# Attention on one Trainium2 core: queries and keys of a pair of heads rounded and split by one operation each, and the last two heads' probabilities turned on TensorE

## The chip, the cores and the metric

The kernel runs on one core of a Trainium2 chip. A core has five engines with instruction queues of their own: TensorE (PE) multiplies matrices, VectorE (DVE) and ScalarE (ACT) work element by element, GpSimd (POOL) and SyncE (SP) here mostly issue transfers, which sixteen DMA engines carry out. The engines meet only at semaphores. On-chip data lies in SBUF, with 128 partitions (rows); TensorE writes to PSUM. The metric is the device time of one execution in microseconds (us). Lower is better.

## The reference

The program is a trunk of four residual layers over 512 tokens of width 1024, in float32: attention, a squared-ReLU MLP, a Griffin recurrent block, another MLP. The change touches attention alone:

```python
qkv = einsum('bsd,de->bse', rmsnorm(h), w_qkv)      # 16 heads of 64
s = einsum('bqhd,bkhd->bhqk', q_c, k_band) * 64**-0.5 + bias
p = softmax(where(key_pos >= 0, s, -1e30))           # own chunk of 64 and the 8 before
o = einsum('bhqk,bkhd->bqhd', p, v_band)
h = h + einsum('bsd,de->bse', o, w_o)
```

With 512 tokens, a query sees all keys up to the end of its own chunk.

## The kernel before

A float32 product is made of three matmuls in a rounded format (fp32r): each operand is split in a high half H (a rounded copy, made on ScalarE) and a low half L (what the rounding left, a subtraction on VectorE), and `mm3` (L288 to L290) adds H·H, L·H and H·L in PSUM. Weights are fetched raw and split in the same way (L179, L184), a few tiles ahead of their use.

Heads go in pairs, since two heads of 64 fill the 128 partitions. A pair p's projected queries and keys come out of `qk_steps`, and `q_out` and `k_out` finish them. `q_out` scales the product to a tile tq (L384), then makes for each head of the pair a 64-row cast (L388) and a 64-row subtraction (L389): a head's q tile has its high half in its own 64 rows and its low half in the other 64. `k_out` scales to tk (L394) and makes four tiles: for each head kh and kl, by a 64-row cast (L399) and subtraction (L400) in the head's own rows; two transfers a head, issued by SyncE (L401, L402), copy them to the other 64 rows. So a score needs only two matmuls a piece: kl against q and kh against q (L483, L484).

`score(h)` makes the scores of head h for four blocks of 128 queries (128 to 512 keys: eight matmuls), adds the bias while taking the maximum (L491, VectorE), takes the exponential and its sum (L498, ScalarE), the reciprocal (L502), divides on ScalarE (L505), turns 32 x 32 blocks on VectorE (L507) and moves the blocks to their places by sixteen transfers (L510), eight issued by SyncE and eight by GpSimd. `split_p(h)` splits these probabilities in pH (L519) and pL (L520). `weigh(h)` multiplies them by v: ten matmuls (L530, L531), then the low and high v halves' results are added (ax L536, o L537), and behind the second head of a pair o is split in oH and oL (L541, L542).

The order is that of a loop over i (from L616 on). Step i makes the scores of head i, fills TensorE with some queued projection work, splits head i-2, weighs head i-3, and fills again. `fill(n)` takes work from one queue: v of pairs 0 to 3 (v0), queries and keys of pairs 2 to 6, v1, queries and keys of pair 7, then the output projection (woA for pairs 0 to 3; wo0, wo1 and woB for pairs 4 to 7). n is FILL up to step 10 and LATE from then on; each item also names the head whose scores or weighing must have been made (`at`). The last output products wait for pair 7: `wo_close` adds it to four opened accumulators. The program's order is the input of the framework's scheduler, which fixes every engine's order when the kernel is built, and may let an instruction pass one that is expected to wait. PSUM has four tiles for projections (tag mm) and four for attention (tag at).

Of the kernel before, what the change touches and what calls it, by code (L numbers as in the profile page):

```python
# [13 lines left out]
ALU = mybir.AluOpType  # L14
# [11 lines left out]
FILL, LATE, LAG = 11.5, 8, 3  # L26
# [9 lines left out]
def f(ap):  # L36
    return ap.bitcast(F32)
# [3 lines left out]
def trunk(ctx: ExitStack, tc: tile.TileContext, xT, cols, gfin, win, wqkv, wo, rwin, rga, rgx, rwo, w1, w2, out):  # L41
# [260 lines left out]
    class Norm:  # L302
# [8 lines left out]
        def square(self, k):  # L311
            if self.acc is None:
                self.both = self.pool.tile([P, 2, T], F32, name=f"{self.name}acc", tag="nn")
                self.acc = self.both[:, 0]
# [14 lines left out]
        def flat(self):  # L329
            ss = atp(f"{self.name}ss")  # L330
            aH, aL = (wk.tile([P, T], F32R, name=f"{self.name}a{i}", tag="nsq", bufs=2) for i in range(2))
            S.copy(aH, self.acc)
            V.tensor_sub(aL, self.acc, f(aH))
            PE.matmul(ss, ones.bitcast(F32R), aH, start=True, stop=False)
            PE.matmul(ss, ones.bitcast(F32R), aL, start=False, stop=True)
            r = self.both[:, 1]
            S.activation(r, ss, AF.Sqrt, bias=epsb, scale=1.0 / D)
            V.reciprocal(r, r)
            return r
# [26 lines left out]
    with ExitStack() as actx:  # L366
# [14 lines left out]

        def q_out(p, acc):
            tmp = wk.tile([P, T], F32, name=f"tq{p}", tag="nsq", bufs=2)
            V.scalar_tensor_tensor(tmp, acc, HD**-0.5, r0, ALU.mult, ALU.mult)  # L384
            for hh in range(2):
                own, oth = HALF[hh], HALF[1 - hh]
                t_ = ab.tile([P, T], F32R, name=f"q{p}{hh}", tag=f"q{hh}", bufs=2)
                S.copy(t_[own], tmp[own])  # L388
                V.tensor_sub(t_[oth], tmp[own], f(t_[own]))  # L389
                q[2 * p + hh] = t_  # L390

        def k_out(p, acc):
            tmp = wk.tile([P, T], F32, name=f"tk{p}", tag="nsq", bufs=2)
            V.tensor_mul(tmp, acc, r0)  # L394
            for hh in range(2):
                own, oth = HALF[hh], HALF[1 - hh]
                kh = ab.tile([P, T], F32R, name=f"kh{p}{hh}", tag=f"kh{hh}", bufs=2)
                kl = ab.tile([P, T], F32R, name=f"kl{p}{hh}", tag=f"kl{hh}", bufs=2)
# [3 lines left out]
                nc.sync.dma_start(f(kl[oth]), f(kl[own]))  # L402
# [70 lines left out]
        def score(h):  # L473
# [11 lines left out]
            for t in range(4):  # L485
                n = (t + 1) * P
                wide = pt[:, seg[t] : seg[t] + n], sc[t], b[:, h % 4, T - n :]
                if t == 1:
# [13 lines left out]
            V.reciprocal(sm, sm)  # L502
            for t in range(4):
# [10 lines left out]
            pts[h] = pt  # L514

        def split_p(h):
            pt = pts.pop(h)
            pH, pL = (a2.tile([P, 10 * P], F32R, name=f"p{n}{h}", tag=f"p{n}", bufs=1) for n in "HL")
            S.copy(pH, pt)  # L519
# [3 lines left out]
        def weigh(h):  # L523
# [3 lines left out]
            for n, (kt, s0, s1, by, t) in enumerate(pieces):  # L527
                vv = vt[p // 2][:, kt, p % 2, 2 * hh : 2 * hh + 2, :].rearrange("p s d -> p (s d)")
                x = oa.rearrange("p (s i a) -> p s i a", i=4, a=32)[:, t : t + len(range(s0, s1, by))]
                PE.matmul(x, vv, pL[:, s0:s1:by], start=n == 0, stop=False, skip_group_check=True)  # L530
                PE.matmul(x, vv, pH[:, s0:s1:by], start=False, stop=n == 4, skip_group_check=True)  # L531
# [51 lines left out]
        def qk(p):  # L583
            return [(f"q{p}", qk_steps(p, q_out), ("s", 2 * p - 3)), (f"k{p}", qk_steps(p, k_out), ("s", 2 * p - 3))]
# [11 lines left out]
        def step():  # L596
            try:
                credit[0] -= next(queue[0][1])
            except StopIteration:
                queue.pop(0)  # L600

        def fill(n):
            credit[0] = min(credit[0], 3) + n
            while credit[0] > 0 and queue and at[queue[0][2][0]] >= queue[0][2][1]:
                step()
# [11 lines left out]
        for i in range(NH + LAG):  # L617
# [11 lines left out]
            if 0 <= i - LAG + 1 < NH:  # L629
                split_p(i - LAG + 1)  # L630
            if 0 <= i - LAG < NH:
                if i - LAG == 13:
                    need("woA")
                need(f"v{(i - LAG) // 8}")
                weigh(i - LAG)
                if i - LAG == 7:
                    residual("h")
                    for k in range(KT):
                        nc.sync.dma_start(hT[k], xT[k * P : (k + 1) * P, :])
                at["w"] = i - LAG  # L640
            fill(n)
        need("woB")
# [645 lines left out]
```

## Time and profile before

| | us |
|---|---|
| median of 3 runs (lowest, highest) | 1032.04 (1030.49, 1032.6) |
| the profiled execution | 1030.76 |
| its span, first to last instruction | 1029.0 |
| attention's stretch in it, about | 25 to 245 |

The mean granted TensorE clock is 0.992 over the span. A row of a timeline has the start, the duration, the engine, the line, the operation, the names of output and inputs, shapes and a count of equal instructions in a row; in brackets stands the time that the engine sat idle ahead of it, and what ended that. SPq is SyncE's queue, PEld TensorE's weight load. A grouped row has the busy time, the mean ns of one, and the idle time ahead of the group by what ended it.

### The profile page before, as it was taken

How to read it: one execution, taken by the hardware profiler on the slowest of the kernel's cores; microseconds unless marked ns; L12 is line 12 of the kernel's file. 1: busy time of each engine (PE TensorE's matmuls, PEld its weight loads, DVE VectorE, ACT ScalarE, POOL GpSimd, SP SyncE). 2: the span in 40 equal slices, each digit the busy share in tenths (PEclk: the TensorE clock that was granted, in tenths of full speed). 3: DMA queues.
4: the chain of work that ended last, by engine and by line, in shares of the span. 5: the costliest groups of instructions: out<-in, count | busy, mean ns of one | idle time of the engine just before them, and what ended most of it. 6: DMA issues, size and time to landing. Idle time of an engine off the chain costs nothing.

```text
span 1029.0 us, 15661 instructions
## 1 busy us (share of the span) xinstructions
PE 1006.7 (98%) x5634; PEld 882.0 (86%) x5634; DVE 865.8 (84%) x1142; ACT 692.5 (67%) x1052; POOL 163.4 (16%) x256
## 2 busy tenths in 40 slices
PE   9998999979999999999999999999999999999997
PEld 8887788768989999999988788888999999999986
DVE  7899988759789898698688989987789798698687
ACT  7688988546786566567567686646686567567565
POOL 1053443313111111111020000003111111111020
PEclk9999999989999999999999999999999999999999
DMA  8476775549838738828673412186838838838572
GB/s 271 125 203 182 196 189 174 132 129 230 240 62 223 208 60 217 215 52 213 204 143 100 129 63 72 52 256 177 223 58 229 206 64 213 214 56 210 144 164 82
DMA packets 135725, 164.15 MB, mean 160 GB/s; under 512 B 10592, under 2 KB 102752, under 8 KB 135648
## 3 DMA queue, kind: packets, MB, share of 16 engines
q1 hardware_dynamic: 108896, 119.43, 37.4%
q0 software_dynamic: 26176, 43.01, 23.2%
q8 instruction: 44, 0.72, 0.3%
q10 hardware_dynamic: 576, 0.72, 0.2%
q14 instruction: 33, 0.27, 0.1%
HBM read 123.27 MB, written 2.10 MB: 122 GB/s over the span
## 4 chain that ended last, share of the span: by engine, by line
PE 75%; DVE 10%; ACT 6%; DMA 5%; issue 2%; SPq 1%; POOL 0%; DVEq 0%; ACTq 0%; POOLq 0%
PE m L290 8%; PE m L289 8%; PE m L288 8%; PE x L288 5%; PE x L289 5%; PE x L290 5%; PE y L289 4%; PE y L288 4%; PE y L290 4%; DVE wl L184 2%; DMA p<-pt 1%; DMA b<-in_w 1%; PE ro L290 1%; PE yb L290 1%; PE yb L288 1%
## 5 line engine op out<-in xcount | busy, mean ns | idle before, releaser
L184 DVE TENSOR_TENSOR wl<-b,wh 128x1024 fp32r<-128x1024 f32 x112 | 135.5, 1220 | 37.1 <-ACT wh L179 37.1
L179 ACT CAST wh<-b 128x1024 fp32r<-128x1024 f32 x112 | 116.7, 1051 | 61.5 <-PE m L289 19.1
L290 PE MATMUL m<-rH,wl 128*128 128x256 f32 x448 | 125.9, 281 | 0.0
L289 PE MATMUL m<-rL,wh 128*128 128x256 f32 x448 | 125.8, 281 | 0.0
L288 PE MATMUL m<-rH,wh 128*128 128x256 f32 x448 | 125.7, 281 | 0.0
L290 PE MATMUL m<-hnH,wl 128*128 128x256 f32 x336 | 95.0, 283 | 0.0
L289 PE MATMUL m<-hnL,wh 128*128 128x256 f32 x336 | 95.0, 283 | 0.0
L288 PE MATMUL m<-hnH,wh 128*128 128x256 f32 x336 | 94.9, 282 | 0.0
L179 ACT CAST wh<-wr 128x1024 fp32r<-128x1024 f32 (+1 forms) x65 | 66.6, 1028 | 38.1 <-PE ro L289 7.0
L289 PEld LDWEIGHTS m<-rL,wh 128*128 128x128 f32 x448 | 85.0, 190 | 1.2
L184 DVE TENSOR_TENSOR wl<-wr,wh 128x1024 fp32r<-128x1024 f32 (+1 forms) x66 | 77.9, 1184 | 9.3 <-ACT wh L179 9.0
L288 PEld LDWEIGHTS m<-rH,wh 128*128 128x128 f32 x448 | 84.8, 189 | 1.0
L290 PEld LDWEIGHTS m<-rH,wl 128*128 128x128 f32 x448 | 84.9, 189 | 0.0
L510 POOL DMA_DIRECT2D p<-pt x128 | 62.8, 499 | 121.8 <-DVE pt L507 70.1
L179 ACT CAST wh<-u 128x1024 fp32r<-128x1024 f32 x56 | 58.2, 1049 | 28.8 <-PE x L290 16.9
L184 DVE TENSOR_TENSOR wl<-u,wh 128x1024 fp32r<-128x1024 f32 x56 | 67.6, 1219 | 3.4 <-ACT wh L179 3.4
L289 PEld LDWEIGHTS m<-hnL,wh 128*128 128x128 f32 x336 | 64.3, 191 | 0.8
L288 PEld LDWEIGHTS m<-hnH,wh 128*128 128x128 f32 x336 | 64.2, 191 | 0.8
L290 PEld LDWEIGHTS m<-hnH,wl 128*128 128x128 f32 x336 | 64.3, 191 | 0.0
L136 POOL DMA_DIRECT2D kept<-in_w x14 | 18.3, 1308 | 261.0 <-DMA wr<-in_w 146.8
L163 POOL DMA_DIRECT2D u<-in_w x14 | 18.4, 1313 | 226.1 <-ACT m L853 117.2
L288 PE MATMUL x<-wh,h 128*128 128x512 f32 (+1 forms) x132 | 51.0, 386 | 0.6 <-DVE d L1062 0.6
(384 smaller groups left out, 3017.5 us busy)
## 6 DMA issues: line engine op xcount, KB each, us to landing
b<-in_w SPq DMA_DIRECT2D x68, 512.0 KB, 6.1
b<-b POOLq DMA_DIRECT2D x36, 512.0 KB, 6.5
kept<-in_w SPq DMA_DIRECT2D x28, 512.0 KB, 3.8
u<-in_w SPq DMA_DIRECT2D x28, 512.0 KB, 6.1
wr<-in_wqkv SPq DMA_DIRECT2D x20, 512.0 KB, 4.8
wr<-in_rwin SPq DMA_DIRECT2D x16, 512.0 KB, 3.6
kept<-in_w POOLq DMA_DIRECT2D x14, 512.0 KB, 7.2
u<-in_w POOLq DMA_DIRECT2D x14, 512.0 KB, 7.5
```

Of the source, the lines that this page charges most:

```text
L136: G.dma_start(four(raw), rows(upper[key]["22"]), accum_op=ALU.add)
L163: G.dma_start(four(raws["us3"]), rows(upper[key]["21"]), accum_op=ALU.add)
L179: high = S.copy(H[:, :n], raw[:, :n])
L184: low = V.tensor_sub(L[:, :n], raw[:, :n], f(H[:, :n]))
L288: PE.matmul(acc, WH, XH, start=start, stop=False, skip_group_check=more)
L289: PE.matmul(acc, WH, XL, start=False, stop=False, skip_group_check=more)
L290: PE.matmul(acc, WL, XH, start=False, stop=stop, skip_group_check=more)
L510: (G if j % 2 else nc.sync).dma_start(pt[32 * j : 32 * j + 32, i * 320 : (i + 1) * 320], turned[32 * i : 32 * i + 32, j].rearrange("p s a ...
```

## The change

It has five parts.

1. `q_out` and `k_out` make one 128-row cast and one 128-row subtraction for a pair (new helper `halves`), where they made two of each over 64 rows. The halves are then carried to their places by transfers (`move`). For k these are six instead of four, on SyncE: the lower 64 rows of the pair's tile a hold head 0, the upper ones head 1; two moves for kh and two for kl copy head 1's rows to both halves of tile b, and only then may one move each copy head 0's rows over the upper rows of tile a. For q there are three, on GpSimd, where there were none; the low half lies in a tile of which there is only one (tag n0), and the third move overwrites rows that the first one reads.
2. The division of `score` is a function of its own (`divide`), which stands behind the second fill of a step.
3. Heads 14 and 15 (from TURNED on) are divided on VectorE by four operations. Ten 128 x 128 transposes on TensorE a head put the probabilities in three PSUM tiles (`turn`), from which three casts and three subtractions make pH and pL. The vector transpose and the sixteen transfers of these two heads are gone. `weigh` takes eight matmuls for them, of 512, 384, 256 and 128 columns.
4. Queries and keys in the fill queue no longer wait to start; only their last step (`out_`) waits for the scores of head 2p-3. The last two heads are split and weighed in the same step of the loop, with a fill between.
5. FILL goes from 11.5 to 11.7, LATE from 8 to 7.5. The norm's two tiles, which were one allocation, are two.

```diff
-FILL, LATE, LAG = 11.5, 8, 3
+FILL, LATE, TURNED = 11.7, 7.5, NH - 2
...
+        def halves(tmp, name, kinds):
+            both = []
+            for n in "hl":
+                t_ = [ab.tile([P, T], F32R, name=f"{name}{n}{i}", tag=k, bufs=1 if k == "n0" else 2) for i, k in enumerate(kinds[n])]
+                both.append(t_)
+            (h, l) = both
+            S.copy(h[0], tmp)
+            V.tensor_sub(l[0], tmp, f(h[0]))
+            return h, l
+
+        def move(queue, dst, i, src, j):
+            queue.dma_start(f(dst[HALF[i]]), f(src[HALF[j]]))
...
-            for hh in range(2):
-                own, oth = HALF[hh], HALF[1 - hh]
-                t_ = ab.tile([P, T], F32R, name=f"q{p}{hh}", tag=f"q{hh}", bufs=2)
-                S.copy(t_[own], tmp[own])
-                V.tensor_sub(t_[oth], tmp[own], f(t_[own]))
-                q[2 * p + hh] = t_
+            (a, b), (low,) = halves(tmp, f"q{p}", {"h": ("q0", "q1"), "l": ("n0",)})
+            move(G, b, 0, a, 1)
+            move(G, b, 1, low, 1)
+            move(G, a, 1, low, 0)
+            q[2 * p], q[2 * p + 1] = a, b
...
+            pairs = halves(tmp, f"k{p}", {"h": ("kh0", "kh1"), "l": ("kl0", "kl1")})
+            for a, b in pairs:
+                move(nc.sync, b, 0, a, 1)
+                move(nc.sync, b, 1, a, 1)
+            for a, b in pairs:
+                move(nc.sync, a, 1, a, 0)
             for hh in range(2):
-                own, oth = HALF[hh], HALF[1 - hh]
...
-                S.copy(kh[own], tmp[own])
-                V.tensor_sub(kl[own], tmp[own], f(kh[own]))
-                nc.sync.dma_start(f(kh[oth]), f(kh[own]))
-                nc.sync.dma_start(f(kl[oth]), f(kl[own]))
-                kk[2 * p + hh] = (kh, kl)
+                kk[2 * p + hh] = tuple(x[hh] for x in pairs)
...
+            while at["s"] < 2 * p - 3:
+                yield 0
             out_(p, acc)
...
+        def divide(h):
+            pt, sm = pts[h]
+            pts[h] = pt
+            if h >= TURNED:
+                for t in range(4):
+                    n = (t + 1) * P
+                    V.tensor_scalar(pt[:, seg[t] : seg[t] + n], pt[:, seg[t] : seg[t] + n], sm[:, t : t + 1], None, ALU.mult)
+                return
...
+        def turn(h, pt, pH, pL):
...
+            for kt in (0, 1, 3, 2):
+                for t in range(kt, 4):
+                    b, c = dst[kt, t]
+                    PE.transpose(b[:, c : c + P], pt[:, seg[t] + kt * P : seg[t] + (kt + 1) * P], ident)
+            for b, c, n in ((x0, 0, T), (x1, T, T), (x2, 2 * T, 2 * P)):
+                S.copy(pH[:, c : c + n], b[:, :n])
+                V.tensor_sub(pL[:, c : c + n], b[:, :n], f(pH[:, c : c + n]))
...
-        for i in range(NH + LAG):
+        for i in range(NH + 2):
...
             fill(n)
-            if 0 <= i - LAG + 1 < NH:
-                split_p(i - LAG + 1)
...
+            if 0 <= i - 2 < NH - 2:
+                split_p(i - 2)
+            if 0 <= i - 3 < NH - 2:
+                weigh_at(i - 3)
             fill(n)
+            if i < NH:
+                divide(i)
+            if i >= NH:
+                split_p(i - 2)
+                fill(n)
+                weigh_at(i - 2)
```

What this does to the engines' orders is shown at three places. The names have the tile's number behind them; a row stands for one or several (x) equal instructions in a row. The line numbers of the kernel before end at L542 in this part; those behind the change are its own (score L495 and L496, probabilities' transfers L532, weighing L576 and L577, moves L392).

SyncE's queue around the keys of pair 2 before: p_589 and p_679 are probabilities of heads 1 and 2 on their way to their places, kh and kl the keys' halves for heads 4 (767, 768) and 5 (773, 774).

```order
L510 DMA p_589<-pt_614 32x320 x8
L375 DMA bias_905<-in_win 128x4x256
L401 DMA kh_767<-kh_767 64x512
L401 DMA kh_773<-kh_773 64x512
L510 DMA p_679<-pt_704 32x320 x8
L402 DMA kl_768<-kl_768 64x512
L402 DMA kl_774<-kl_774 64x512
```

And now (k2h and k2l are the high and low halves of pair 2's keys, 752 and 754 the tiles a of head 4, 753 and 755 the tiles b of head 5):

```order
L532 DMA p_594<-pt_683 32x320 x8
L154 DMA wr_1079<-in_wqkv 128x8x128
L392 DMA k2h_753<-k2h_752 64x512 x2
L392 DMA k2l_755<-k2l_754 64x512 x2
L374 DMA bias_923<-in_win 128x4x256
L392 DMA k2h_752<-k2h_752 64x512
L392 DMA k2l_754<-k2l_754 64x512
L532 DMA p_704<-pt_790 32x320 x8
```

All of pair 2's keys are now ahead of the eight p transfers that stood between kh and kl.

SyncE's queue around the keys of pair 7 before (p_1956 are head 13's probabilities, wr raw weights):

```order
L510 DMA p_1888<-pt_1913 32x320 x8
L401 DMA kh_2090<-kh_2090 64x512
L510 DMA p_1956<-pt_1981 32x320 x8
L402 DMA kl_2091<-kl_2091 64x512
L401 DMA kh_2096<-kh_2096 64x512
L402 DMA kl_2097<-kl_2097 64x512
L154 DMA wr_2309<-in_wo 128x4x256
```

And now (p_1971 are head 13's probabilities):

```order
L532 DMA p_1971<-pt_2046 32x320 x8
L392 DMA k7h_2108<-k7h_2107 64x512 x2
L392 DMA k7l_2110<-k7l_2109 64x512 x2
L154 DMA wr_2320<-in_wo 128x4x256
L392 DMA k7h_2107<-k7h_2107 64x512
L392 DMA k7l_2109<-k7l_2109 64x512
L154 DMA wr_2443<-in_w 128x8x128
```

Here all six stand behind the eight p transfers, a weight transfer between the first hop and the second.

TensorE around the last head's weighing before (wo are accumulators of the output projection, oH_2426 pair 7's output):

```order
L290 MATMUL wo_2490<-oH_2389,wl_2274 128x512
L530 MATMUL oa_2412<-pL_2394,v_1664 128x256
L531 MATMUL oa_2412<-pH_2393,v_1664 128x256
L530 MATMUL oa_2412<-pL_2394,v_1664 128x256
L531 MATMUL oa_2412<-pH_2393,v_1664 128x256
L530 MATMUL oa_2412<-pL_2394,v_1664 128x384
L531 MATMUL oa_2412<-pH_2393,v_1664 128x384
L530 MATMUL oa_2412<-pL_2394,v_1664 128x128
L531 MATMUL oa_2412<-pH_2393,v_1664 128x128
L530 MATMUL oa_2412<-pL_2394,v_1664 128x256
L531 MATMUL oa_2412<-pH_2393,v_1664 128x256
L288 MATMUL wo_2436<-oH_2426,wh_2235 128x512
```

And now from head 14's transposes on (p_2122 and x_2372 to x_2374 are head 14's probabilities before and behind them, oa_2391 its output; p_2172 and x_2406 are head 15's):

```order
L546 MATMUL x_2372<-ident,p_2122 128x128 x4
L546 MATMUL x_2373<-ident,p_2122 128x128 x4
L546 MATMUL x_2374<-ident,p_2122 128x128 x2
L288 MATMUL wo_2501<-oH_2161,wh_2250 128x512
L289 MATMUL wo_2501<-oL_2162,wh_2250 128x512
L290 MATMUL wo_2501<-oH_2161,wl_2251 128x512
L288 MATMUL wo_2447<-oH_2366,wh_2193 128x512
L576 MATMUL oa_2391<-pL_2371,v_1611 128x512
L577 MATMUL oa_2391<-pH_2370,v_1611 128x512
L546 MATMUL x_2406<-ident,p_2172 128x128
L576 MATMUL oa_2391<-pL_2371,v_1611 128x384
L577 MATMUL oa_2391<-pH_2370,v_1611 128x384
```

Head 14 is weighed four matmuls behind its transposes, with head 15's transposes in between the pieces; behind head 15's weighing pair 7's products follow in both kernels, at once before, and two matmuls later now.

More of the change, by code (lines that the diff above doesn't have):

```diff
@@ L487, in score @@
                 wide = pt[:, seg[t] : seg[t] + n], sc[t], b[:, h % 4, T - n :]
-                if t == 1:
+                if t == 1 and h < TURNED:
                     wide = [x.rearrange("p (k c) -> p k c", k=2) for x in wide]
@@ L513, in score @@
                     )
-            pts[h] = pt
+        def turn(h, pt, pH, pL):
+            x0, x1, x2 = atp(f"x0{h}"), atp(f"x1{h}"), atp(f"x2{h}")
+            dst = {(0, t): (x0, t * P) for t in range(4)}
+            dst.update({(1, t): (x1, (t - 1) * P) for t in range(1, 4)})
+            dst.update({(2, t): (x2, (t - 2) * P) for t in range(2, 4)})
+            dst[3, 3] = (x1, 3 * P)
+            for kt in (0, 1, 3, 2):
[5 more added lines that the diff above has]
+                V.tensor_sub(pL[:, c : c + n], b[:, :n], f(pH[:, c : c + n]))
         def split_p(h):
@@ L597, in step @@
             try:
-                credit[0] -= next(queue[0][1])
+                n = next(queue[0][1])
             except StopIteration:
                 queue.pop(0)
+                return True
+            credit[0] -= n
+            return n > 0
         def fill(n):
             credit[0] = min(credit[0], 3) + n
-            while credit[0] > 0 and queue and at[queue[0][2][0]] >= queue[0][2][1]:
-                step()
+            while credit[0] > 0 and queue and at[queue[0][2][0]] >= queue[0][2][1] and step():
+                pass
         def need(name):
@@ L616, in trunk, with weigh_at @@
         credit[0] = 0
-        for i in range(NH + LAG):
+        def weigh_at(h):
+            if h == 13:
+                need("woA")
+            need(f"v{h // 8}")
+            weigh(h)
+            if h == 7:
+                residual("h")
+                for k in range(KT):
+                    nc.sync.dma_start(hT[k], xT[k * P : (k + 1) * P, :])
+            at["w"] = h
+        for i in range(NH + 2):
             n = FILL if i < 11 else LATE
```

39 lines of the change are left out of this document (19 added, 20 removed).

## The prediction

> **What bounds the kernel now.** I read the busy table of the page first, then TensorE's timeline from 20 to 250 us (the change touches attention alone), then windows around the waits that I found there, and last SyncE's queue and ScalarE's timeline at those places.
>
> ```profile
> PE 1006.7 (98%) x5634; PEld 882.0 (86%) x5634; DVE 865.8 (84%) x1142; ACT 692.5 (67%) x1052; POOL 163.4 (16%) x256
> ```
>
> TensorE is busy 98% of the span, so a change to the other engines is worth only what it takes out of TensorE's waits. These are the waits of over 1 us in attention (in brackets the idle time ahead of an instruction and what ended it), with three rows between them that give the pace:
>
> ```profile
> 79.52 0.30 PE L483 MATMUL s<-kl,q 128*128 128x128 f32 x1 [1.67 <-DMA kl<-kl]
> ...
> 101.89 0.50 PE L483 MATMUL s<-kl,q 128*128 128x512 f32 x1 [1.04 <-DVE mx L491]
> ...
> 120.17 0.30 PE L483 MATMUL s<-kl,q 128*128 128x128 f32 x1 [1.61 <-issue]
> ...
> 159.94 0.33 PE L530 MATMUL oa<-pL,v 128*128 128x128 f32 x1 [1.12 <-DVE v L432]
> ...
> 176.51 0.39 PE L288 MATMUL wo<-oH,wh 128*128 128x512 f32 x1
> ...
> 187.39 0.39 PE L288 MATMUL wo<-oH,wh 128*128 128x512 f32 x1
> 189.48 0.30 PE L483 MATMUL s<-kl,q 128*128 128x128 f32 x1 [1.71 <-DMA kl<-kl]
> ...
> 221.63 0.58 PE L530 MATMUL oa<-pL,v 128*128 128x256 f32 x1 [3.65 <-DVE pL L520]
> ...
> 226.39 2.08 PE L288 MATMUL wo<-oH,wh 128*128 128x512 f32 x4 [2.04 <-ACT oH L541]
> ...
> 231.64 0.39 PE L288 MATMUL wo<-oH,wh 128*128 128x512 f32 x1
> ```
>
> The seven waits sum to 12.84 us. From 176.51 to 187.39 stand 48 matmuls, so one takes 0.227 us; four at 226.39 took 2.08 instead of 0.91. The windows say why (columns: window, its length, busy time of PE, PEld, DVE, ACT and POOL, granted TensorE clock, DMA share, GB/s):
>
> ```profile
> 100.00:125.00 25.00, 22.35 (x110) 18.23 (x109) 23.92 (x46) 22.36 (x49) 13.99 (x29) 1.00 0.73 204
> 190.00:195.00 5.00, 5.00 (x25) 4.78 (x24) 2.08 (x10) 2.80 (x9) 0.00 (x0) 0.66 1.03 305
> 220.00:225.00 5.00, 2.72 (x10) 2.42 (x10) 1.50 (x2) 0.63 (x2) 0.00 (x0) 0.63 0.00 0
> 225.00:230.00 5.00, 3.61 (x9) 2.83 (x10) 2.02 (x3) 0.83 (x2) 0.00 (x0) 0.50 0.33 100
> ```
>
> Behind the waits of 189, 221 and 226 us TensorE works at 0.66, 0.63 and 0.50 of its clock. What that costs is busy time by the missing share: 5.00 x 0.34 + 2.72 x 0.37 + 3.61 x 0.50 = 4.5 us, and perhaps 0.8 more up to 231.64: 5.3 us. So 18 us is all that any change here can win back.
>
> **The change part by part.**
>
> *Two of the waits are for kl.* SyncE's queue shows that kl stands behind the eight p transfers of a head (pair 2, then pair 7; the row has the start of the issues and their sum):
>
> ```profile
> 70.98 6.02 SPq L510 DMA_DIRECT2D p<-pt  x8
> 77.10 1.18 SPq L402 DMA_DIRECT2D kl<-kl  x2
> ...
> 181.75 5.18 SPq L510 DMA_DIRECT2D p<-pt  x8
> 187.04 0.53 SPq L402 DMA_DIRECT2D kl<-kl  x1
> ```
>
> ```profile
> DMA to landing us min/median/max: 2.2/2.3/4.3
> ```
>
> An issue takes 1.18/2 = 0.59 us and kl lands 2.3 us later: 77.10 + 2.3 = 79.4, which is the wait at 79.52. Every k now needs six transfers, four and then two that wait for the first ones to land. For pair 2 all six are now ahead of the p transfers: 77.10 minus the start of those eight, 70.98, is 6.1 us; two more issues (1.2) and a second landing with its wait (2.3) take 3.5 of them. Both kl's are there some 2.6 us earlier than before, against a wait of 1.67. That wait goes: **-1.7**.
>
> For pair 7 all six stand behind head 13's eight p transfers. By the rows of before: four issues from 187.04 to 189.4, the second hop's wait to about 191.5, its landing at 193.8, that is 17.3 us behind 176.51. TensorE asks for it later than before: 82 matmuls stand ahead of it instead of 49, 82 x 0.227 = 18.6 us. A margin of 1.3 us, of which I expect 1 to 2 to be lost, since pair 7's k is now computed late in the vector queue. I take a wait of 0.5 in place of 1.71; the ends are 0 and 2.5 (one landing of 4.3 instead of 2.3, less half the margin).
>
> For pair 0 the second hop adds 2.9 us (issue and landing); head 0's scores stand ten matmuls later (2.3 us). Nothing here shows how much slack k0 had, so the cost is between 0 and 0.6; I take 0.3.
>
> The three q transfers of a pair go to GpSimd's queue, which is busy 16% of the span, and which loses the 16 p transfers of two heads. They wait for ScalarE's cast and the vector subtraction, and behind them the bias copies and p transfers of that queue wait too, by some 2.4 us a pair; q is computed far ahead of its use except in pair 7. I take 0.
>
> *The vector engine while it is full.* From 100 to 125 us it is busy 23.92 of 25. The waits at 101.89 and 120.17 belong to it: score pieces there queue for vector work of projections. What a pair saves:
>
> ```profile
> L389 DVE TENSOR_TENSOR q<-tq,q 64x512 fp32r<-64x512 f32 x16 | 11.1, 692 | 0.5
> ...
> L542 DVE TENSOR_TENSOR oL<-o,oH 128x512 fp32r<-128x512 f32 x8 | 5.4, 675 | 1.5 <-ACT oH L541 1.4
> ```
>
> A subtraction of 64 rows takes 692 ns, of 128 rows 675. A pair needs two instead of four: -1.38 us of vector time, the same number of casts less on ScalarE. Off this stretch nothing waits for it. In it 1.38 us a pair is about the size of one of the two waits (1.04, 1.61), but divisions now also queue elsewhere. I count half of 2.65: **-1.3**, with ends 0 and -2.65.
>
> *The wait for v at 159.94.* In the new order head 12's scores stand ahead of that group: 2,560 columns, 5 x 0.227 = 1.1 us of matmuls; of 1.12 I count **-0.9** (ends 0 and -1.1).
>
> *The tail.* Head 15's probabilities decide it (ScalarE's timeline):
>
> ```profile
> 207.90 1.92 ACT L505 ACTIVATE p<-p,sm 128x128 f32<-128x128 f32 x4
> ...
> 218.79 1.26 ACT L519 CAST pH<-p 128x1280 fp32r<-128x1280 f32 x1 [2.91 <-DMA p<-pt]
> ...
> 224.39 0.58 ACT L536 COPY ax<-oa 64x512 f32<-64x512 f32 x1 [4.34 <-PE oa L531]
> 225.72 0.62 ACT L541 CAST oH<-o 128x512 fp32r<-128x512 f32 x1 [0.76 <-DVE o L537]
> ```
>
> Dividing starts at 207.90, but the cast starts at 218.79: the vector transpose and the sixteen transfers take most of 11 us. The change replaces them by ten TensorE transposes a head, whose price another stage shows:
>
> ```profile
> 553.25 1.04 PE L997 MATMUL back<-ident,d 128*128 128x128 f32 x8
> 554.04 0.47 PE L288 MATMUL x<-wh,h 128*128 128x512 f32 x1
> ```
>
> Eight take 554.04 - 553.25 = 0.79 us, so twenty take 2.0: **+2.0**, all of it on TensorE. The division on the vector engine has no row; by 675 ns for 512 columns of two operands, 1280 columns take 1.7 us, by ScalarE's row 1.92; nothing but the transposes waits for it, and the vector transpose that goes makes room. So head 15's transposed p is split some 7 us earlier than before, and its wait of 3.65 goes. What is late next:
> - Head 14's weighing now stands close behind its own transposes. A first part needs cast and subtraction, 0.62 + 0.68 = 1.3 us, and each of the two others 0.68 more, against 0.6 us of transposes and four matmuls (0.9) ahead and pieces of some 0.4 between: I take 2.0 for heads 13 to 15 together (ends 0.5 and 4).
> - The last product still needs ax, o and oH of head 15: 0.58 + 0.69 + 0.62 = 1.9 us, of which two matmuls cover 0.45: 1.5 instead of 2.04.
> - The clock: 1.7 us of waiting at 189 was enough for 0.66 behind it, so I keep 1.5 of the 5.3 us (ends 0 and 4).
>
> From 176.51 to 231.64 are 55.1 us. Less the waits of 1.71, 3.65 and 2.04 and the clock's 5.3, that leaves 42.4. After: 42.4 + 2.0 + 0.5 + 2.0 + 1.5 + 1.5 = 49.9: **-5.2**.
>
> **Sum:** -1.7 + 0.3 - 1.3 - 0.9 - 5.2 = -8.8, call it -9. The profiled execution took 1030.76 us (span 1029.0): 1030.76 - 9 = 1021.8. It lies 1.28 below the median of the runs, 1032.04, so on their scale I predict **1023**. Behind 231.64 the order of work is as before, with the same matmuls and TensorE at work throughout, so I expect the gain to be carried to the end; FILL and LATE change by 0.2 and 0.5 of a credit, and act by the places counted above.
>
> **The rivals.**
> - *The clock does not follow.* The tail keeps short waits, and the clock stays low behind them: 4 us instead of 1.5, and half a microsecond of waits more. That is 3 less of gain: 1026. For it: 1.7 us of waiting at 189 us did it. Against it: nothing waits 3.65 any more. The Trainium skill ("TensorE: Matmul & The Clock Gate", Part 4: PE-mode transpose) says that transposes do not count as TensorE being busy in the same way and that the full clock does not engage for them; by that rule this rival gains. At 553.25 the trace does not agree: the 512-column matmuls behind eight transposes keep their pace.
> - *Nearly all waits go.* The forecast keeps 0.3 + 1.3 + 0.2 + 0.5 + 2.0 + 1.5 + 1.5 = 7.3 us of waits and lost clock. If 4 of them go too: -13, 1019. For it: the vector and scalar engines are relieved by more than the waits measure. Against it: the tail is one chain (transposes, split, product, split), with little beside it.
> - *The waits only change places.* Division now stands behind the second fill, so each head's transpose, transfers and split start later, and a wait of 0.5 us at each of a dozen weighings takes 6 of 9: 1029 to 1031. For it: the order. Against it: only head 15 waited for p by more than 1 us on TensorE.
> - *Slower: the two hops land late.* At 4.3 instead of 2.3 us a hop, each of the three tight chains (pair 0, 2, 7) ends 4 us later; less margins of 0.5, 2.6 - 1.7 = 0.9 and 0.8 that is 9 us, and 3 of clock behind them: +3, 1035. It decides from hops of some 3 us on. For it: the maximum of 4.3 is in the trace, and DMA share was 1.03 at 190 us. Against it: the median is 2.3, the minimum 2.2. The Trainium skill ("DMA: Bandwidth & Descriptors", Rules for kernel authors) says that two transfers to disjoint halves of the partitions only serialize, since they share the same engines, and to use one; with its ceiling of 435 GB/s (Bandwidth) a transfer of 128 KB is 0.3 us, and four together end 0.9 us after one, an estimate that would make 1024 of 1023. No row here has four such transfers at once.
>
> **How the numbers follow.** Forecast 0.49 (its own range 1020 to 1025), clock 0.22, nearly all waits go 0.12, only change places 0.10, slower 0.07. The range reaches from 1016.5 (vector waits, tail and clock all at their better ends) into the fourth case, 1030.5, and leaves out the slower one and the ends. A measurement of this kernel tells about 0.2%, 2.1 us, from no change: below 1030.0 is faster, above 1034.1 slower. Faster 0.84, within 0.2% 0.09, slower 0.07.
>
> **What would show it.** Right: no kl wait ahead of head 4's scores; under 1 us ahead of head 14's; head 15's weighing no longer behind a wait of over 2 us; 20 transposes of about 0.1 us; the first matmul behind the last product 8 to 10 us earlier than 231.64. Wrong: a wait for k of pair 0, 2 or 7 over 1 us, landings of k or q over 3 us, waits for pL spread over all heads, a granted clock under 0.7 from the transposes to the end of attention, or new idle time behind 232 us.

## The result and the profile after

The changed kernel takes 1041.88 us (median of 4 runs, 1041.16 to 1043.23), the kernel before beside it 1031.88 (4 runs). The ratio is 1.010, with an interval from 1.0083 to 1.0118: about 10 us slower. The prediction was 1023, with a range up to 1030.5.

The page after, its span and busy times:

```profile
span 1040.3 us, 15658 instructions
...
PE 1012.9 (97%) x5650; PEld 884.7 (85%) x5650; DVE 854.7 (82%) x1136; ACT 677.7 (65%) x1032; POOL 166.0 (16%) x264
```

VectorE is busy 11.1 us less and ScalarE 14.8 us less than before, as the change intends. The span is 11.3 us longer all the same. TensorE's timeline after, with the waits over 1.4 us in attention, one of 1.36 in the MLP, and four marks (first output product 189.53, head 14's transposes 225.16, first product behind the four closed accumulators 239.33, first product of the MLP 250.21):

```profile
44.03 0.30 PE L495 MATMUL s<-k0l,q0h 128*128 128x128 f32 x1 [2.04 <-DMA k0l<-k0l]
...
85.02 0.30 PE L495 MATMUL s<-k2l,q2h 128*128 128x128 f32 x1 [2.95 <-DMA k2l<-k2l]
...
131.22 0.44 PE L495 MATMUL s<-k4l,q4h 128*128 128x128 f32 x1 [2.75 <-issue]
...
170.20 0.33 PE L576 MATMUL oa<-pL,v 128*128 128x128 f32 x1 [1.74 <-DVE v L444]
...
179.41 0.39 PE L576 MATMUL oa<-pL,v 128*128 128x256 f32 x1 [1.85 <-DVE o L583]
...
189.53 0.39 PE L288 MATMUL wo<-oH,wh 128*128 128x512 f32 x1
...
209.72 0.30 PE L495 MATMUL s<-k7l,q7h 128*128 128x128 f32 x1 [1.45 <-DMA k7l<-k7l]
...
225.16 1.25 PE L546 MATMUL x<-ident,p 128*128 128x128 f32 x10
...
236.47 1.20 PE L288 MATMUL wo<-oH,wh 128*128 128x512 f32 x4 [1.53 <-ACT oH L587]
...
239.33 0.39 PE L288 MATMUL wo<-oH,wh 128*128 128x512 f32 x1
...
250.21 0.39 PE L288 MATMUL u<-hnH,wh 128*128 128x512 f32 x1
...
303.80 0.50 PE L289 MATMUL y<-wl,hs 128*128 128x512 f32 x1 [1.36 <-DVE wl L184]
```

In both kernels 820 matmuls stand ahead of the first output product and 4556 from the first MLP product on (between them 258 before and 274 after, by the twenty transposes and four weighing matmuls fewer), so these two marks cut the span in three. The first MLP product before:

```profile
242.57 0.39 PE L288 MATMUL u<-hnH,wh 128*128 128x512 f32 x1
```

**A** reaches to the first output product, **B** from there to the first MLP product, **C** to the end:

| | A | B | C | span |
|---|---|---|---|---|
| before | 176.5 | 66.1 | 786.4 | 1029.0 |
| after | 189.5 | 60.7 | 790.1 | 1040.3 |
| difference | +13.0 | -5.4 | +3.7 | +11.3 |

So the tail of attention, B, won what was forecast for it (-5.2). The loss is in A, where 3.6 us were to be won, and some in C, where nothing was to change. A window of 35 to 40 us, and the four stretches of A in which the granted clock is low (columns as before):

```profile
35.00:40.00 5.00, 5.00 (x23) 4.13 (x22) 1.76 (x4) 1.57 (x3) 1.04 (x2) 1.00 1.02 243
45.52:48.93 3.41, 3.41 (x10) 2.64 (x9) 1.27 (x7) 1.58 (x6) 0.00 (x0) 0.50 0.25 55
86.48:89.89 3.41, 3.41 (x10) 2.64 (x9) 3.01 (x9) 1.43 (x6) 2.80 (x6) 0.50 0.67 167
130.85:134.27 3.42, 3.06 (x10) 2.80 (x11) 2.03 (x8) 0.65 (x1) 3.42 (x8) 0.50 0.82 215
171.81:175.23 3.42, 3.42 (x10) 2.64 (x9) 0.75 (x2) 0.21 (x1) 1.59 (x5) 0.50 1.09 369
```

The five waits of A sum to 11.33 us, and with four of them goes a clock of 0.50 for 3.4 us: by busy time and missing share 1.7 + 1.7 + 1.5 + 1.7 = 6.6 us. Together 17.9. Before, A had waits of 5.44 us (1.67, 1.04, 1.61, 1.12), and the granted clock was 1.00 in every window from 20 to 175 us. The difference, 12.5, is nearly all of the 13.0. The first row tells something else: from 35 to 40 us the DMA engines are full (share 1.02), just where pair 0's halves are on their way.

The chain of waits shows how (start, duration, what). Pair 0, then pair 2:

```profile
33.95 0.69 DVE k0l L388
...
35.81 5.64 DMA k0l<-k0l
41.51 2.39 DMA k0l<-k0l
44.03 0.30 PE s L495
```

```profile
71.99 0.27 ACT k2h L387
...
75.62 5.08 DMA k2l<-k2l
80.75 4.13 DMA k2l<-k2l
...
85.02 0.30 PE s L495
```

A key now goes through two transfers, and the second starts when the first has landed. The prediction took 2.3 us for a landing, the median of before. Pair 0's first hop took 5.64 us and pair 2's two took 5.08 and 4.13. TensorE's first score of head 4 starts 0.14 us behind the second landing. The three transfers of each low half, from issue to landing (k0l, then k2l):

```profile
DMA to landing us min/median/max: 2.4/5.1/5.6
```

```profile
DMA to landing us min/median/max: 4.1/5.1/5.3
```

The profile before already had a late landing at this place: pair 2's two kh transfers, issued from 69.33 on, took 4.3 us each.

### The profile page after: what moved, and what is told of

It is laid out like the page before. It is cut to its first block, busy times and chain, and to the rows that moved or that the text cites. A ratio compares the mean times of both kernels' runs of the same rounds, so it can differ in the third digit from the quotient of the medians.

```text
span 1040.3 us, 15658 instructions
## 1 busy us (share of the span) xinstructions
PE 1012.9 (97%) x5650; PEld 884.7 (85%) x5650; DVE 854.7 (82%) x1136; ACT 677.7 (65%) x1032; POOL 166.0 (16%) x264
## 4 chain that ended last, share of the span: by engine, by line
PE 75%; DMA 8%; DVE 7%; ACT 6%; SPq 2%; issue 2%; POOL 0%; DVEq 0%; ACTq 0%
PE m L290 9%; PE m L288 9%; PE m L289 9%; PE x L288 6%; PE x L289 6%; PE x L290 6%; PE y L289 4%; PE y L288 4%; PE y L290 4%; ACT p L510 2%; DMA wr<-in_wqkv 2%; DVE wl L184 2%; PE ro L290 1%; PE yb L288 1%; PE ro L289 1%
## 5 line engine op out<-in xcount | busy, mean ns | idle before, releaser
L179 ACT CAST wh<-wr 128x1024 fp32r<-128x1024 f32 (+1 forms) x65 | 66.6, 1027 | 45.2 <-DMA wr<-in_wo 11.3
L184 DVE TENSOR_TENSOR wl<-u,wh 128x1024 fp32r<-128x1024 f32 x56 | 67.6, 1218 | 4.8 <-ACT wh L179 4.8
L532 POOL DMA_DIRECT2D p<-pt x112 | 54.8, 497 | 59.8 <-DVE mx L507 31.0
```

Of the source, the lines that this page charges most:

```text
L179: high = S.copy(H[:, :n], raw[:, :n])
L184: low = V.tensor_sub(L[:, :n], raw[:, :n], f(H[:, :n]))
L532: (G if j % 2 else nc.sync).dma_start(pt[32 * j : 32 * j + 32, i * 320 : (i + 1) * 320], turned[32 * i : 32 * i + 32, j].rearrange("p s a ...
```

## The experiments

Each kernel changes the one named; "old" is as in the kernel before. Medians and ratios are against the kernel before, run on the same chip. A, B and C come from each kernel's one profiled execution, and scatter with it: the kernel before alone took 1029.2 to 1035.7 us in the 25 runs beside the first four kernels. So a difference of a few us in A is an indication, and the medians have to agree with it. The profiled executions of qk_only and first_old are the shortest of their four.

| kernel | us | ratio [interval] | A | B | C |
|---|---|---|---|---|---|
| qk_only | 1050.2 | 1.018 [1.014, 1.023] | 187.7 | 67.6 | 787.9 |
| k_old | 1030.9 | 0.999 [0.997, 1.001] | 185.7 | 57.5 | 786.5 |
| q_old | 1035.8 | 1.004 [1.002, 1.005] | 185.9 | 61.1 | 787.5 |
| qk_old | 1027.2 | 0.996 [0.994, 0.997] | 182.0 | 57.7 | 786.1 |
| tail_only | 1022.1 | 0.991 [0.987, 0.994] | 176.3 | 57.6 | 785.7 |
| divide_old | 1029.3 | 0.998 [0.997, 1.000] | 178.8 | 58.1 | 790.7 |
| gate_old | 1023.5 | 0.992 [0.988, 0.995] | 178.0 | 58.6 | 785.6 |
| k_one_hop | 1030.8 | 0.999 [0.997, 1.000] | 182.0 | 59.2 | 788.1 |
| q0_old | 1027.2 | 0.994 [0.993, 0.996] | 180.5 | 57.5 | 787.5 |
| bias_moved | 1031.8 | 1.000 [0.998, 1.001] | 185.5 | 58.8 | 785.9 |
| tail_one_hop | 1037.1 | 1.005 [1.003, 1.007] | 186.7 | 60.0 | 788.3 |
| first_old | 1037.8 | 1.006 [1.004, 1.009] | 186.5 | 59.9 | 785.3 |

### Which part of the change costs

**k_old**: the changed kernel with `k_out` of before.

```diff
-            pairs = halves(tmp, f"k{p}", {"h": ("kh0", "kh1"), "l": ("kl0", "kl1")})
...
+                S.copy(kh[own], tmp[own])
+                V.tensor_sub(kl[own], tmp[own], f(kh[own]))
+                nc.sync.dma_start(f(kh[oth]), f(kh[own]))
+                nc.sync.dma_start(f(kl[oth]), f(kl[own]))
```

> The changed kernel with the keys made as before (64-row casts and subtractions, four single transfers a pair); queries and all else as changed. Theory hops (the second hop of a key, landing some 5 us after its issue while weights are loading, costs most of the 13 us that are lost ahead of the first output product): the waits for k0l and k2l go (2.04 and 2.95 us, and 1.7 us of low clock behind each), 1034 to 1036 us. Rival queries (the three query transfers on GpSimd's queue hold the bias copies and the one low tile): no better than 1039. Rival order (division behind the second fill, the earlier start of projections, FILL and LATE): 1038 or more.

It took 1030.9, 11 us less, where the theory gave 6 to 8. Neither rival holds alone, but A is still 3.7 us longer than with both old (185.7 against 182.0).

**q_old**: the changed kernel with `q_out` of before.

```diff
-            (a, b), (low,) = halves(tmp, f"q{p}", {"h": ("q0", "q1"), "l": ("n0",)})
-            move(G, b, 0, a, 1)
-            move(G, b, 1, low, 1)
-            move(G, a, 1, low, 0)
...
+                S.copy(t_[own], tmp[own])
+                V.tensor_sub(t_[oth], tmp[own], f(t_[own]))
```

> The changed kernel with the queries made as before (64-row operations, no transfers); keys and all else as changed. Theory hops: the waits for k0l and k2l stay above 1.5 us, 1038 to 1041 us, a part won back at head 9's scores alone (2.75 us now, behind a late bias copy). Rival queries: 1034 or less, and the waits for k0l and k2l under 1 us, since fewer transfers are under way. Rival order: 1039 or more.

It took 1035.8, 6 us less, so the queries cost something too. Head 4's scores still wait for k2l (1.93 us instead of 2.95), and head 0's for k0l (1.77 instead of 2.04); the wait of 2.75 us at head 9's scores is gone.

**qk_old**: both of before.

```diff
-            (a, b), (low,) = halves(tmp, f"q{p}", {"h": ("q0", "q1"), "l": ("n0",)})
...
-            pairs = halves(tmp, f"k{p}", {"h": ("kh0", "kh1"), "l": ("kl0", "kl1")})
```

> The changed kernel with keys and queries both as before; turned heads, division, starts, FILL and LATE as changed. Theories hops and queries: the 13 us ahead of the first output product go, the tail keeps its 5 us and the MLP behind it gives back up to 4: 1027 to 1031 us. Rival order: the rest costs too, 1035 or more, with waits over 1.5 us at scores or weighings ahead of the output products.

1027.2: faster than before. In A, keys cost 185.7 to 189.5 or 182.0 to 185.9 (3.9 us either way) and queries 185.9 to 189.5 or 182.0 to 185.7 (3.7): in these profiles they add up, 7.6 of the 13.0. The other 5.5 (182.0 against 176.5) belong to the rest of the change. Over the whole time keys and queries cost 14.7 us together (1041.9 against 1027.2), keys the larger part: beside A's 7.6, B is 3.0 and C 4.0 us shorter without them.

**qk_only**: the other way round, the kernel before with only the new keys and queries.

```diff
-                S.copy(t_[own], tmp[own])
-                V.tensor_sub(t_[oth], tmp[own], f(t_[own]))
...
+            (a, b), (low,) = halves(tmp, f"q{p}", {"h": ("q0", "q1"), "l": ("n0",)})
...
+            pairs = halves(tmp, f"k{p}", {"h": ("kh0", "kh1"), "l": ("kl0", "kl1")})
```

> The kernel before with only the new keys and queries (one operation for 128 rows, halves carried by transfers) and the two norm tiles apart. Theories hops and queries: slower than before by 8 to 14 us, with waits for k0l and k2l. Rival order: within 3 us of before, since the new halves only hurt together with the moved division and the earlier projections.

19 us slower, more than expected. In the old order k2l was waited for 4.10 us and k5l for 2.86, in the profile of its shortest run.

### What in the rest costs, and what the tail is worth

**tail_only**: the kernel before with the turned heads and the new end of the loop.

```diff
-FILL, LATE, TURNED = 11.7, 7.5, NH - 2
+FILL, LATE, TURNED = 11.5, 8, NH - 2
...
                 score(i)
+                divide(i)
...
-            while at["s"] < 2 * p - 3:
-                yield 0
...
-            if i < NH:
-                divide(i)
```

> The kernel before with only the turned last heads and the shorter loop (keys, queries, place of the division of heads 0 to 13, starts, FILL and LATE as before). Theory order (division behind the second fill, the earlier starts and FILL cost the 5.5 us by which the first output product is later with old keys and queries than before): first output product at 176 to 178 us, tail of 47 to 50 us, 1020 to 1024 us. Rival: those 5.5 us come from the turned heads or the loop's new end themselves, through the scheduler: first output product at 180 us or later, 1026 to 1029.

(The diff is against qk_old.) 1022.1, the fastest kernel here, 0.9% faster than before. A is that of before (176.3), B is 8.4 us shorter. The mean granted clock is 0.999 instead of 0.992: behind the turned heads TensorE waits nowhere over 0.4 us up to the MLP.

**divide_old** and **gate_old** put back one half each of what tail_only puts back.

```diff
                 score(i)
+                divide(i)
...
-            if i < NH:
-                divide(i)
```

> The changed kernel with old keys and queries, and the division of a head at once behind its exponential again (starts, FILL and LATE as changed). If the place of the division costs the 5.5 us ahead of the first output product: that product at 177 to 178 us, 1021 to 1024. If the starts and FILL do: no change from 1027, product at 181 to 183.

```diff
-FILL, LATE, TURNED = 11.7, 7.5, NH - 2
+FILL, LATE, TURNED = 11.5, 8, NH - 2
...
-            while at["s"] < 2 * p - 3:
-                yield 0
...
-            return [(f"q{p}", qk_steps(p, q_out), ("s", -1)), (f"k{p}", qk_steps(p, k_out), ("s", -1))]
+            return [(f"q{p}", qk_steps(p, q_out), ("s", 2 * p - 3)), (f"k{p}", qk_steps(p, k_out), ("s", 2 * p - 3))]
```

> The changed kernel with old keys and queries, and with starts, FILL and LATE as before (division behind the second fill as changed). The other half of the same question: if starts and FILL cost the 5.5 us, the first output product at 177 to 178 us and 1021 to 1024; if the place of the division does, no change from 1027.

Neither expectation fits cleanly. Against tail_only the moved division alone costs 1.7 us in A (gate_old), the starts and FILL alone 2.4 (divide_old), both together 5.7 (qk_old). In the total, the starts and FILL are the larger: 1029.3 against 1022.1, of which 5.0 lie in C; with both the loss in C is gone again. These differences in A are within what single profiles scatter by. Which of the starts, FILL and LATE does it was not tried.

### Why keys and queries cost

**k_one_hop**: against q_old, the keys' one cast and one subtraction go to tiles of their own, and eight transfers, none of which waits for another, carry the halves.

```diff
-            pairs = halves(tmp, f"k{p}", {"h": ("kh0", "kh1"), "l": ("kl0", "kl1")})
-            for a, b in pairs:
-                move(nc.sync, b, 0, a, 1)
-                move(nc.sync, b, 1, a, 1)
-            for a, b in pairs:
-                move(nc.sync, a, 1, a, 0)
...
+                for x, y in ((kh, h), (kl, l)):
+                    move(nc.sync, x, 0, y, hh)
+                    move(nc.sync, x, 1, y, hh)
```

> The changed kernel with old queries, and keys rounded and split by one operation each over 128 rows into separate tiles, from which eight transfers a pair carry the halves, none of which waits for another (with two hops: 1035.8, first output product at 185.9; with old keys: 1027.2 and 182.0). Theory second hop: it goes, the waits for k0l and k2l under 0.7 us, 1027 to 1030. Rival traffic (the transfers of keys are slow because more of them run beside weights): eight are worse than six, 1036 or more, and the waits for k0l and k2l stay over 1.5 us.

More transfers, but A falls from 185.9 to 182.0. Heads 0 and 4, which waited 1.77 and 1.93 us with two hops, start their scores on TensorE's timeline almost without a wait:

```profile
40.58 0.30 PE L488 MATMUL s<-kl,q 128*128 128x128 f32 x1 [0.18 <-DMA kl<-tk]
...
79.12 0.22 PE L488 MATMUL s<-kl,q 128*128 128x128 f32 x1
```

So with the new order the second hop, and not the number of transfers, is what these two waits come from. That A is that of the old keys (182.0 as well) is in part chance: other waits differ, as 4.14 us at 176.12 here. In the total some of it stays, 1030.8 against 1027.2 (B and C are 1.5 and 2.0 longer).

**q0_old**: k_old, with the queries of pair 0 alone made as before.

```diff
+            if p == 0:
+                for hh in range(2):
...
+                    S.copy(t_[own], tmp[own])
+                    V.tensor_sub(t_[oth], tmp[own], f(t_[own]))
...
+                return
```

> The run with old keys (k_old: 1030.9 us, first output product at 185.7), and the queries of pair 0 alone made as before too. Theory late first queries (at the start of attention the chain of q0's transfers lands behind three weight loads and holds head 0's scores, 1.66 us and then a low clock, and the low tile for q1, 4.3 us of the vector engine): the wait goes, first output product at 182 to 183 us, 1027 to 1029, as with all queries old. Rival GpSimd's queue (bias copies behind the query transfers of pairs 3 and 5): no change, 1030 or more.

1027.2: all that queries cost beside old keys goes with pair 0's. k_old's chain of waits shows one part of it; the third query transfer waits for the first one, and both land late:

```profile
31.79 4.45 DMA q0h<-q0h
...
36.52 5.22 DMA q0h<-q0l
...
41.98 0.30 PE s L496
```

That wait is 1.66 us, and no low clock follows it (1.00 from 41.98 to 48.80), unlike what was expected. A larger part went elsewhere: k_old waits 2.74 us at head 9's scores, with a clock of 0.50 for 3.4 us behind, and q0_old does not wait there. How pair 0's queries bring that about is not shown.

**bias_moved**: k_old, with the bias copies on ScalarE and the bias memset on VectorE. They stand behind query transfers on GpSimd in the changed kernel:

```profile
125.86 0.52 POOL L392 DMA_DIRECT2D q5h<-q5l  x1 [0.22 <-issue]
128.25 0.53 POOL L392 DMA_DIRECT2D q5h<-q5l  x1 [1.87 <-DMA p<-pt]
128.77 1.42 POOL L376 COPY bias<-bias 128x256 f32<-128x256 f32 x4
```

VectorE's first maximum of head 8 then waits for the bias, and TensorE's head 9 starts at 131.22, 0.11 us behind the end of the second one (in k_old and gate_old it is 0.10 to 0.11 us as well), which frees a PSUM tile:

```profile
130.47 0.29 DVE L503 CUSTOM_DVE_ANT_0 p<-s,bias 128x128 f32<-128x128 f32 x1 [1.25 <-POOL bias L377]
...
131.03 0.08 DVE L503 DVE_READ_ACCUMULATOR2_ANT mx<- 128x1 f32 x1
```

```diff
-                G.tensor_copy(b[:, h, 0 : 2 * P], b[:, h, 2 * P : 2 * P + 1].to_broadcast([P, 2 * P]))
-            G.memset(b[0:HD, :, T - HD :], NEG)
+                S.copy(b[:, h, 0 : 2 * P], b[:, h, 2 * P : 2 * P + 1].to_broadcast([P, 2 * P]))
+            V.memset(b[0:HD, :, T - HD :], NEG)
```

> The run with old keys (k_old), with the bias copies on ScalarE and the bias memset on VectorE in place of GpSimd, so that they no longer stand behind query transfers. Rival GpSimd's queue: the wait of 2.74 us at head 9's scores falls under 1.5, and 1028 to 1029 us. Theory late first queries: within 1 us of 1030.9.

The wait at head 9's scores fell from 2.74 to 1.65 us, but that for q0 grew from 1.66 to 3.69, and the time is the same. This is inconclusive: the bias is part of head 9's wait, and the total doesn't show it. The query transfers are not needed for that wait: gate_old has none, and waits 3.37 us there, VectorE 2.02 of them for the bias.

**first_old**: the changed kernel, with pair 0's keys and queries as before.

```diff
+            if p == 0:
+                for hh in range(2):
...
+                    kk[2 * p + hh] = (kh, kl)
+                return
```

> The changed kernel with queries and keys of pair 0 alone made as before; pairs 1 to 7 with two hops and transfers as changed. Theory start and pair 2 (with old keys, pair 0's queries were the whole cost of the queries; what keys cost beside them is the second hop of pairs 0 and 2): the 2.04 us at head 0's scores and the low clock behind it go, the wait for k2l stays at 1.5 to 3 us, first output product at 184 to 187 us instead of 189.5, 1035 to 1038. Rival: everything came from the start, 1030 or less, k2l's wait under 1 us. Other rival: the start does not matter with two-hop keys, 1040 or more.

1037.8, 4 us less than the changed kernel, with A at 186.5: head 0 waits no more, and k2l is waited for 3.30 us (hops of 5.29 and 4.57 us). By A pair 0 is 3.0 of the 7.6 us. Its four runs scatter by 7 us, and the profiled one is the shortest, so A bears only this coarse reading: pair 0 is a part, and not all.

**tail_one_hop**: tail_only with the one-hop keys.

```diff
-                nc.sync.dma_start(f(kh[oth]), f(kh[own]))
-                nc.sync.dma_start(f(kl[oth]), f(kl[own]))
...
+                    move(nc.sync, x, 0, y, hh)
+                    move(nc.sync, x, 1, y, hh)
```

> The kernel before with the turned heads (tail_only, 1022.1 us) and the one-hop keys: one cast and one subtraction a pair, eight transfers, none waiting for another. If fewer vector operations are worth what the prediction gave them (1.3 us) and a key's transfer costs only by its hop: 1019 to 1022, the waits of 1.04 and 1.61 us at 101 and 120 us shorter. If eight transfers a pair cost SyncE's queue more (four more issues, 2.4 us a pair): 1023 or more, with longer waits for keys of pairs 2 and 7.

1037.1, 15 us slower than tail_only. In the old order the eight transfers stand among the p transfers on SyncE, and heads 4 and 8 wait 2.02 and 3.14 us for their keys. One hop is no cure by itself: what cost nothing in A beside old queries in the new order costs 10 us of A in the old one. That the p transfers hold the keys up is read from the order, no run separates it. The wait of 1.04 us at 101 us is gone, as the vector time saved would have it; it does not make up for the rest.

## Why the prediction was wrong

In the medians the turned tail won some 10 us (tail_only), the moved division, the starts, FILL and LATE cost 5 of them (qk_old against tail_only), and the new keys and queries 15 more (the changed kernel against qk_old). The prediction gave the tail 5, the rest nothing, and the keys and queries a gain.

- **"All six are now ahead of the p transfers ... That wait goes: -1.7"**: wrong. This is the step that failed first. All six were ahead, but the step used 2.3 us for a landing, the median of a range of 2.2 to 4.3. The landings of pair 2 took 5.08 and 4.13 us (DMA share 1.03 from 75 to 80 us), so the wait became 2.95 instead of 0, and the clock fell behind it. For pair 0 I took 0.3 us; it was 2.04 and a low clock of 1.7.
- **"The three q transfers ... I take 0"**: wrong. Queries cost 3.7 us of A (q_old, and qk_old against k_old) and 4 to 6 us of the medians. The reason given, that q is computed far ahead of its use, named pair 7 as the exception; beside old keys pair 0 is the one (q0_old), since its queries are needed at once. Beside two-hop keys, q_old left most of head 0's wait, shortened pair 2's and took away pair 4's, so where the cost lies there is open.
- **The vector engine, -1.3**: not seen. VectorE works 11 us less, but its time was not the limit: the waits that VectorE seemed to end in A are not fewer after. The wait at 120.17, read as a queue for a full VectorE, was in part VectorE's own wait of 0.51 us for the bias from GpSimd.
- **The wait for v, -0.9**: wrong, 1.74 us instead of 1.12.
- **"FILL and LATE ... act by the places counted above"**, and the moved division as a rival of 6 us: with old keys and queries these parts cost 5.5 us of A. They had no term in the sum.
- **The tail, -5.2**: right in size (-5.4 in B; 49.8 us from the first output product to the mark at 239.33, where 49.9 were forecast), and the mechanism too: the long wait for head 15's probabilities is gone. That it fits so closely is luck. Ten transposes take 1.01 us to the next matmul's start, as forecast, and the last wait is 1.53 instead of 1.5. But pair 7's key is waited for 1.45 us instead of 0.5; around heads 13 to 15 one wait of 1.15 (at 228.26, for an oH and not for a weighing) stands for the 2.0; and the clock, where 1.5 us were kept, stayed full. In the seven kernels with old keys and turned heads B is 7.3 to 8.6 us shorter than before.
- **"I expect the gain to be carried to the end"**: wrong by 3.7 us. Weight transfers for the MLP start 0.7 us behind the first product with pair 7's output (226.39 before, 236.47 after); in the profiles before and after (SyncE, then ScalarE):

```profile
227.14 0.93 SPq L134 DMA_DIRECT2D kept<-in_w  x2
...
279.85 1.05 ACT L179 CAST wh<-u 128x1024 fp32r<-128x1024 f32 x1 [1.78 <-DMA u<-in_w]
```

```profile
237.21 0.92 SPq L134 DMA_DIRECT2D kept<-in_w  x2
...
289.86 1.05 ACT L179 CAST wh<-u 128x1024 fp32r<-128x1024 f32 x1 [3.21 <-DMA u<-in_w]
```

They start 10.1 us later, the first MLP product (242.57 and 250.21) only 7.6: a lead of 13.0 us instead of 15.4. ScalarE then waits 3.21 us for a weight instead of 1.78, and TensorE 1.36 at 303.80, with a clock of 0.50 from 304.93 to 308.35 behind it (1.7 us more). In all fourteen profiles C goes with that wait of ScalarE: where it was 2.35 us or more, C is 787.5 to 790.7, where it was 1.78 or less or not there, 785.3 to 786.5. Of the seven kernels with the long wait TensorE waits 1.2 to 1.4 us in each; the two in which the clock falls behind it (the changed kernel and divide_old) have 790.1 and 790.7, the others 787.5 to 788.3. The lead sets it only in part (six kernels have 13.0, and first_old among them does not wait). This is a comparison, not a test: no run moved these transfers alone.

Of the rivals, the slower one happened: "the two hops land late", given 0.07, at pair 0 and pair 2 as it said, at pair 7 less (k7l's hops took 2.35 and 3.76 us; 1.45 us of wait where 0.5 was taken). All three waits for k are over the 1 us that was named as a sign of being wrong. The rival's price, +3, lacked the queries, the rest of the change and C. The maximum of 4.3 was in a quoted row, and the landings of over 5 us quoted above lie where the DMA engines are full (1.02 and 1.03): I read the DMA share at 190 us and in the window from 100 to 125, not at the first and third pair's keys. "No row here has four such transfers at once" misses the kernel before itself: pair 0's four, issued from 35.03 to 36.91 at a share of 0.66 (35 to 38 us), landed in 2.3 to 2.4 us each. So four together are not late by their number.

Three numbers of the prediction need a correction that does not change the outcome. Its clocks of 0.66 and 0.63 are means of 5-us windows; the clock was 0.50, from 190.61 to 194.03 and from 221.33 to 231.57, which makes 5.7 us and not 5.3. The range's lower end, 1016.5, does not come out of the ends given for its terms: vector waits, tail and clock at their better ends make about 1018. The slower rival's three times 4 us less 2.2 is 9.8, not 9.

The wait at 179.41 ends behind VectorE, which had itself waited for a weight of the output projection (landed at 175.00, cast on ScalarE) before it came to the split and the sum that TensorE needed:

```profile
170.11 4.89 DMA wr<-in_wo
```

```profile
176.10 1.23 DVE L184 TENSOR_TENSOR wl<-wr,wh 128x1024 fp32r<-128x1024 f32 x1 [3.54 <-ACT wh L179]
```

What stays open: what makes a landing late (it goes with full DMA engines, but no run took the other transfers away), which of the starts, FILL and LATE costs, where the queries cost beside two-hop keys, and why the weight of the MLP is waited for 3.30 us in divide_old and 1.31 in qk_old.

## What to carry to other kernels

A transfer that waits for another is priced by landings under load at that place, not by the median of the run, and counted at the first use after start-up too, where nothing runs ahead. Saving time on an engine that is not the limit is worth nothing if it is paid for in latency on the chain that feeds the limiting engine; try the parts of such a change one by one, since here one part (the turned last heads with the new end of the loop, 0.991) was good and the others ate it. When a tail gets shorter, look at what was loading behind it.

## What the runs showed of the hardware

- A transfer of 128 KB within SBUF landed 2.3 us after its issue in the median of before (kl, shares of 0.58 and 0.66 where it was looked at), and 5.08 to 5.64 us after it where the DMA engines were full (share 1.02 from 35 to 40 us, 1.03 from 75 to 80). The share over the landing alone does not tell: the second hop of k0l took 2.39 us at 0.82.
- The granted clock falls to 0.50 for 3.4 us (or two or three times that: 6.8 in k_old from 109.63, 10.2 before from 221.33), and the length of a wait on TensorE alone does not decide about it. It fell with waits of 1.74, 2.04, 2.75 and 2.95 us after the change and of 1.71 before; it stayed at 1.00 behind 1.85 (179.41), in tail_only behind 1.67, in first_old behind 3.30 (81.94) and in gate_old behind 3.37 (121.97). What else decides is not shown.
- Twenty transposes, the first ten in a row (1.01 us from the first to the next matmul), did not lower the clock: it was 1.00 in every window from 225 to 240 us. The Trainium skill ("TensorE: Matmul & The Clock Gate", Part 4: PE-mode transpose) says that transposes don't count as busy in the same way; no trace here shows that.
